# A hybrid decoder layer on one core: rows of the stationary operands at pitches over 1024 bytes

## The chip, the cores and the metric

The kernel runs on one core of a Trainium2 chip. The metric is the device time of one execution in microseconds. TensorE (PE) multiplies: for each matmul a weight load puts 128 columns of a stationary operand into the array, and then up to 512 columns of a moving operand stream through it; the result goes to a bank of PSUM. VectorE (DVE), ScalarE (ACT) and GpSimd (POOL) work elementwise, SyncE (SP) and POOL issue the loads. All operands of the engines lie in SBUF, 128 partitions of some 224 KiB; a place in it is given here as a byte within the partition.

## The reference

One layer on 256 tokens of width 1024, all in float32. Attention (8 heads of 64, causal within one block of 256 tokens) and a convolution module stand side by side, and a SwiGLU feed-forward of width 2816 follows:

```python
h = rms_norm(x, norm1_g[l])
proj = h @ w_in[l]                                  # 1024 x 2560
q, k, v, u = jnp.split(proj, [ATTN_WIDTH, 2 * ATTN_WIDTH, 3 * ATTN_WIDTH], axis=-1)
...
attn = moba_attention(...)                          # one block: causal softmax attention
conv = conformer_conv(u, ...)                       # GLU, 31-tap causal depthwise conv, layer norm, silu
x = x + jnp.concatenate([attn, conv], axis=-1) @ w_out[l]
h = rms_norm(x, norm2_g[l])
x = x + (jax.nn.silu(h @ w_gate[l]) * (h @ w_up[l])) @ w_down[l]
```

## The kernel before, in words

Every float32 product is made of three float32r products: each operand is split into a rounded high part and a rest (`xh`/`xl`, `mixh`/`mixl`, `wh`/`wl` and so on), and `high*high`, `high*low` and `low*high` are summed in PSUM (line 698 in the first projection, `product` with line 735 in all later ones). The activations are the stationary operands, in 128x128 blocks (one k-tile of 128 features by one of the two halves of the tokens), and the weights are the moving ones, 512 columns at a time. One matmul is therefore 128x512, and there are six for each k-tile and 512 columns of weights.

The stages in order, with the names of their results in PSUM and of their stationary operands:

- `p`: the first projection, 5 chunks of 512 columns, 8 k-tiles, 240 matmuls on `xh`, `xl` (line 698). The work of attention and convolution runs beside it in small tasks that a step counter starts: scores `S`, transposes `qT`, `kT`, `pT`, the convolution's spectrum `hf` on the constant `fwd` (lines 296 to 298).
- `O` (attention's output) and `cv` (the convolution's inverse transform, on the constant `inv`, lines 296 to 298, and one matmul on `tapr`, line 648).
- `po`: the output projection, 96 matmuls on `mixh`, `mixl`. These reuse the memory of `xh`, `xl` (tags `big_h`, `big_l`).
- `fg`, `U`, `V`, `W`: gate and up projections. The feed-forward's input is `g2` (high parts in `ffn["h"]`, rests in `ffn["l"]`, 8 rows each). Two of the six column blocks are done plainly (`fg`, 144 matmuls); the other four as seven products instead of eight of 2x2 blocks (`shared_unit`, `U`, `V`, `W`): three of the seven take blocks of `g2` (144 matmuls), the other four take sums and differences of blocks, `xs` (192 matmuls). In before, two of the four sums lie in the last four rows of `act`, which are filled only at the end, and two in a tile of their own, so half of these matmuls carry the name `act` in the profile.
- `pd`: the down projection, 264 matmuls on `act`, the split and transposed activations (22 rows of high parts, 22 of rests).

The order of the matmuls is written out (`TURNS`, `_order`), with the down projection's rows between the shared products. The weights come in 1 MB blocks (`raw`), from SP's queue; ACT makes `wh` (line 273) and DVE `wl` (line 278), some pieces ahead (`feed`). For the shared products POOL's queue adds one block of weights to another in memory (line 286). `SCRATCH` is the room, in bytes of each partition, that is set aside at the start of SBUF for the descriptors of POOL's queue.

The weight load of a matmul runs while the matmul ahead of it streams. In before all rows of the stationary operands have a pitch of 1024 bytes (256 float32), their two token halves lie 512 bytes apart, and every piece of weights starts 320 bytes over a multiple of 1024, in steps of 2048:

| tile | start, modulo 512 | pitch of its rows | place against the moving operand, modulo 512 |
|---|---|---|---|
| `wh`, `wl` (moving) | 320 | 2048 (halves) | - |
| `xh`, `xl`, `mixh`, `mixl`, `g2`, `act`, `xs` | 320 | 1024 (`xs`: 512) | 0 |
| `fwd`, against `hh`, `hl` | 416 | 1024 | 96 |
| `inv`, against `yh`, `yl` | 384 | 1024 | 64 (32 where `tapr` is next) |

Of the kernel before, what the change touches and what calls it, by code (L numbers as in the profile page):

```python
# [9 lines left out]
F32R = mybir.dt.float32r  # L10
# [6 lines left out]
P = 128  # L17
D = 1024
T = 256
NT = T // P  # L20
KT = D // P
# [4 lines left out]
NF = FF // P  # L26
# [25 lines left out]
LATE = (1, 5)  # L52
SECOND = 3
SCORES = 8
SCRATCH = 8192
GLU0_WAIT = 3
L1 = 8
L2 = 28
# [129 lines left out]
def build(nc, tc, t):  # L188
    with ExitStack() as ctx:
        _build(nc, tc, t, ctx)  # L190
    keep_order(nc, tc)


def _build(nc, tc, t, ctx):
    pool = lambda name, bufs=1, **kw: ctx.enter_context(tc.tile_pool(name=name, bufs=bufs, **kw))
    const = pool("const")
    keep = pool("keep")
# [6 lines left out]
    def mm_bank(name, two):  # L204
        return psum.tile([P, 512], F32, name=name, tag=f"mm{two}", bufs=2)
# [34 lines left out]
    def load(i):  # L240
        if i in homes:
            pl = late_pool[0] if homes[i] == "side" else keep
            r = pl.tile([P, BW], F32, name=f"raw{i}", tag=homes[i])
        else:
            r = raw.tile([P, BW], F32, name=f"raw{i}", tag="raw")
        nc.sync.dma_start(r, t["w"][i - 2])
        blocks[i] = r
# [94 lines left out]
        nc.tensor.matmul(warm[:, 0:T], zeros[:, 0:P], zeros, start=True, stop=True)  # L342


    xh = keep.tile([P, KT, T], F32R, name="xh", tag="big_h")
    xl = keep.tile([P, KT, T], F32R, name="xl", tag="big_l")
    def split_x(kt):
        nc.scalar.activation(xh[:, kt, :], xT[kt], AF.Copy, scale=g1[:, kt:kt + 1])
        yield
        nc.vector.scalar_tensor_tensor(xl[:, kt, :], xT[kt], g1[:, kt:kt + 1], xh[:, kt, :].bitcast(F32),  # L350
                                       op0=ALU.mult, op1=ALU.subtract)
        yield
# [40 lines left out]
    G = {}  # L393
# [311 lines left out]
    nc.scalar.activation(vs[:, 0, :], banks[0], AF.Copy, scale=rstd1[:, 0:1])  # L705
    nc.scalar.activation(vs[:, 1, :], banks[1], AF.Copy, scale=rstd1[:, 1:2])
    G["third"]()
    mix = G["mix"] = [keep.tile([P, KT, T], F32R, name="mix" + s, tag="big_" + s) for s in "hl"]
    O = [mm_bank(f"O{n}", 1).rearrange("p (a q) -> p a q", a=2) for n in range(2)]
    for second in range(2):  # L710
        step()
        for i in range(NT):
            for n in range(2):
                for odd in range(2):
                    h = 4 * n + 2 * second + odd
# [12 lines left out]
    ffn = {"r": None}  # L728
# [41 lines left out]
    at = 20  # L770
# [7 lines left out]
        at += 1  # L778
    early_ctx.close()
    late = ffn["late"] = late_pool[0] = pool("late")  # L780
    xg = late.tile([P, 2, KT, T], F32R, name="g2")
    ffn["h"], ffn["l"] = xg[:, 0], xg[:, 1]
    ffn["full"] = late.tile([P, KT, T], F32, name="full", tag="side")
    for n in range(2):
        for i in range(NT):
# [8 lines left out]
    spawn(turn_task(1), TURN_WAIT)  # L794


    acts = late.tile([P, 2, NF, T], F32R, name="act")
    load(first_shared[0])
    load(first_shared[2])

# [41 lines left out]
    def part(name):  # L842
        return late.tile([P, W], F32, name=name, tag="sum", bufs=4)

    more = late.tile([P, 2, 2, 4, P], F32R, name="xs")
    spare = [acts[:, z, NF - 4:, :].rearrange("p f (b q) -> p (f b) q", b=2).rearrange("p (s k) q -> p s k q", s=2)
             for z in range(2)]
    xs = [[(spare[z], more[:, z])[j // 2][:, j % 2] for j in range(4)] for z in range(2)]

    def xsums_task():  # L850
        a = ffn["full"]
# [178 lines left out]
```

## Time and profile before

| | |
|---|---|
| median of 2 runs | 283.17 us (282.84 and 283.5) |
| the profiled execution's own time | 282.85 us |
| its span, first to last instruction | 281.1 us |
| granted TensorE clock, mean | 1.000 |
| matmul records | 1302 |
| weight loads of pd from act (min/median/max) | 187/188/190 ns |
| ACT's wh, each 128x1024 | 1057 ns |
| DVE's wl, each 128x1024 | 1220 ns |
| packets of POOL's queue | 2848, 9.94 MB |

The span is what the trace covers; the execution's own time holds a little more around it. "Busy" of PE counts each matmul from its start to the modelled end of its drain, which overlaps the next one: a matmul of 389 ns does not hold the array for 389 ns. What counts is the distance from one start to the next, and that is read from the timeline's starts or from the chain of waits, whose rows give the time that a run of matmuls took and their number.

### The profile page before, as it was taken

The numbers are of one execution on the slowest core, as the hardware profiler recorded it, in microseconds if no ns is written. First come the engines' busy times: TensorE is split into PE (matmuls) and PEld (weight loads), VectorE is DVE, ScalarE is ACT, GpSimd is POOL, SyncE is SP. The second block draws the span as 40 slices with busy tenths as digits, with TensorE's granted clock in tenths as the row PEclk, the third lists the DMA queues.
The fourth block names the chain that finished last, engine by engine and source line by source line (L and its number), as shares of the span: only waits on it lengthen the run. The fifth ranks groups of instructions, "written<-read, shape, count | busy, mean of one in ns | idle before, by whom it ended". The sixth has DMA issues, their size and how long they took to land.

```text
span 281.1 us, 3712 instructions
## 1 busy us (share of the span) xinstructions
PE 276.5 (98%) x1302; PEld 225.8 (80%) x1302; DVE 238.5 (85%) x353; ACT 188.6 (67%) x280; POOL 30.5 (11%) x54
## 2 busy tenths in 40 slices
PE   8999999999999999999999999999999999999995
PEld 5878887888788888888888888888888888888883
DVE  3889998898994957999998999989998999978412
ACT  6768577998838778664887559765687568954300
POOL 0004555002000000011200012001110022000000
PEclk9999999999999999999999999999999999999999
DMA  7999967655543689349999689997699985910012
GB/s 240 412 415 325 411 217 266 239 215 161 223 150 149 234 295 368 133 169 212 264 243 361 266 209 193 349 426 215 108 177 423 373 189 96 328 58 2 0 53 97
DMA packets 13029, 65.12 MB, mean 232 GB/s; under 512 B 1841, under 2 KB 2705, under 8 KB 7250
## 3 DMA queue, kind: packets, MB, share of 16 engines
q1 hardware_dynamic: 9874, 54.80, 51.6%
q0 software_dynamic: 2848, 9.94, 19.0%
q8 instruction: 10, 0.16, 0.2%
q10 hardware_dynamic: 288, 0.14, 0.2%
q14 instruction: 9, 0.07, 0.1%
HBM read 63.63 MB, written 1.05 MB: 230 GB/s over the span
## 4 chain that ended last, share of the span: by engine, by line
PE 92%; DMA 4%; DVE 1%; issue 1%; SPq 0%; ACT 0%; DVEq 0%
PE pd L735 21%; PE U L735 16%; PE p L698 15%; PE fg L735 12%; PE po L735 8%; PE V L735 8%; PE W L735 4%; DMA c_gqk<-gqk 3%; PE aT L816 2%; DMA first<-first 1%; PE S L533 1%; PE O L717 1%; PE pT L567 1%; PE x2T L758 1%; PE cv L296 0%
## 5 line engine op out<-in xcount | busy, mean ns | idle before, releaser
L273 ACT ACTIVATE wh<-raw 128x1024 fp32r<-128x1024 f32 x114 | 117.8, 1057 | 35.8 <-DVE raw L272 19.9
L278 DVE TENSOR_TENSOR wl<-raw,wh 128x1024 fp32r<-128x1024 f32 x114 | 136.0, 1220 | 5.4 <-ACT wh L273 4.5
L735 PE MATMUL pd<-wh,act 128*128 128x512 f32 x176 | 58.0, 394 | 0.0
L735 PEld LDWEIGHTS pd<-wh,act 128*128 128x128 f32 x176 | 33.0, 188 | 6.8
L735 PE MATMUL pd<-wl,act 128*128 128x512 f32 x88 | 34.3, 389 | 0.0
L698 PE MATMUL p<-wh,xh 128*128 128x512 f32 x80 | 32.7, 408 | 0.0
L698 PE MATMUL p<-wh,xl 128*128 128x512 f32 x80 | 31.3, 391 | 0.0
L286 POOL DMA_DIRECT2D raw<-w x16 | 14.1, 880 | 157.7 <-PE fg L735 60.8
L735 PE MATMUL fg<-wh,g 128*128 128x512 f32 x96 | 30.4, 391 | 0.0
L698 PE MATMUL p<-wl,xh 128*128 128x512 f32 x80 | 26.6, 394 | 0.1
L735 PE MATMUL U<-wh,g 128*128 128x512 f32 x64 | 21.5, 393 | 0.0
L735 PEld LDWEIGHTS fg<-wh,g 128*128 128x128 f32 x96 | 18.0, 188 | 3.7
L272 DVE TENSOR_TENSOR raw<-raw,raw 128x1024 f32<-128x1024 f32 x16 | 19.5, 1219 | 0.1
L735 PEld LDWEIGHTS pd<-wl,act 128*128 128x128 f32 x88 | 16.6, 188 | 3.3
L735 PE MATMUL fg<-wl,g 128*128 128x512 f32 x48 | 18.7, 390 | 0.0
L698 PEld LDWEIGHTS p<-wh,xh 128*128 128x128 f32 x80 | 15.1, 189 | 3.8 <-issue 0.7
L698 PEld LDWEIGHTS p<-wl,xh 128*128 128x128 f32 x80 | 15.0, 189 | 3.7 <-DVE wl L278 0.7
L698 PEld LDWEIGHTS p<-wh,xl 128*128 128x128 f32 x80 | 15.0, 188 | 3.1
L819 ACT ACTIVATE act<-aT 128x512 fp32r<-128x512 f32 (+1 forms) x12 | 6.7, 560 | 12.9 <-PE aT L816 12.9
L735 PEld LDWEIGHTS U<-wh,g 128*128 128x128 f32 x64 | 12.0, 188 | 2.4
L735 PE MATMUL po<-wh,mixh 128*128 128x512 f32 x32 | 12.6, 395 | 0.0
L735 PE MATMUL po<-wh,mixl 128*128 128x512 f32 x32 | 12.5, 390 | 0.0
(184 smaller groups left out, 443.9 us busy)
## 6 DMA issues: line engine op xcount, KB each, us to landing
raw<-w SPq DMA_DIRECT2D x45, 1024.0 KB, 7.2
raw<-w POOLq DMA_DIRECT2D x16, 512.0 KB, 7.0
first<-first SPq DMA_DIRECT2D x8, 384.0 KB, 5.9
xtok<-xtok SPq DMA_DIRECT2D x2, 512.0 KB, 9.1
x<-xtok SPq DMA_DIRECT2D x2, 512.0 KB, 6.4
inv<-inv POOLq DMA_DIRECT2D x1, 768.0 KB, 5.3
out<-o SPq DMA_DIRECT2D x3, 256.0 KB, 2.0
c_glub<-glub SPq DMA_DIRECT2D x1, 512.0 KB, 10.4
```

Source lines behind the costliest of these rows:

```text
L272: nc.vector.tensor_tensor(src, src, blocks[add][:, cut(a)], op=ALU.add)
L273: nc.scalar.activation(dst[0], src, AF.Copy)
L278: nc.vector.tensor_tensor(dst[1], src, dst[0].bitcast(F32), op=ALU.subtract)
L286: nc.gpsimd.dma_start(blocks[to][:, cut(a)], t["w"][more - 2][:, cut(a)], accum_op=ALU.add)
L533: nc.tensor.matmul(banks[2 * j + a][:, out], G["qT"][rows, j, q], G["kT"][rows, j, k], start=True, stop=True)
L567: nc.tensor.transpose(b[:, a * P:(a + 1) * P], p[:, a * P:(a + 1) * P], ident)
L698: nc.tensor.matmul(banks[i], (xh, xh, xl)[a][:, kt, sls[i]], w[a % 2], start=kt == 0 and a == 0, stop=kt == KT - 1 and a == 2 - (order[-1] ...
L717: nc.tensor.matmul(o, vs[:, i, h * HD:(h + 1) * HD], G["pT"][h][:, i * T:i * T + T - i * P], start=i == 0, stop=i == 1)
L735: nc.tensor.matmul(bank, l, r, start=start and a == 0, stop=stop and a == 2, skip_group_check=on)
L758: nc.tensor.transpose(b[:, a, tok(i)], x2[:, i, k * P:(k + 1) * P], ident)
L816: nc.tensor.transpose(b[:, a, :], u[:, a * P:(a + 1) * P], ident)
L819: nc.scalar.activation(hi, b[:, 0:nf, :], AF.Copy)
```

## The change

Five rows of constants are new, and a helper `spaced` makes a tile whose rows of 256 elements have a number of unused elements behind each (and, for `mix`, 64 ahead of the first). `xh`, `xl` and `mix` get 8 (a pitch of 1056 bytes), `g2` gets 1 (1028 bytes), `act` gets 4 (1040 bytes). The four shared sums lie in a tile of their own, `more`, with rows of 512 bytes; the last rows of `act` are no longer lent to them. The room for POOL's descriptors is halved. Nothing is computed in another way, and the order of the instructions on all five engines is the same; only the names and places of operands differ.

```diff
-SCRATCH = 8192
+SCRATCH = 4096
+X_PAD = 8
+MIX_PAD = 8
+MIX_AT = 64
+G_PAD = 1
+ACT_PAD = 4
...
-    xh = keep.tile([P, KT, T], F32R, name="xh", tag="big_h")
-    xl = keep.tile([P, KT, T], F32R, name="xl", tag="big_l")
+    def spaced(pl, name, rows, pad, at=0, dt=F32R, **kw):
+        tl = pl.tile([P, at + rows * (T + pad)], dt, name=name, **kw)
+        return tl[:, at:].rearrange("p (k q) -> p k q", k=rows)[:, :, 0:T]
+
+    xh = spaced(keep, "xh", KT, X_PAD, tag="big_h")
+    xl = spaced(keep, "xl", KT, X_PAD, tag="big_l")
...
-    mix = G["mix"] = [keep.tile([P, KT, T], F32R, name="mix" + s, tag="big_" + s) for s in "hl"]
+    mix = G["mix"] = [spaced(keep, "mix" + s, KT, MIX_PAD, MIX_AT, tag="big_" + s) for s in "hl"]
...
-    xg = late.tile([P, 2, KT, T], F32R, name="g2")
-    ffn["h"], ffn["l"] = xg[:, 0], xg[:, 1]
+    xg = spaced(late, "g2", 2 * KT, G_PAD)
+    ffn["h"], ffn["l"] = xg[:, 0:KT], xg[:, KT:]
...
-    acts = late.tile([P, 2, NF, T], F32R, name="act")
+    acts = spaced(late, "act", 2 * NF, ACT_PAD).rearrange("p (z f) q -> p z f q", z=2)
...
-    more = late.tile([P, 2, 2, 4, P], F32R, name="xs")
-    spare = [acts[:, z, NF - 4:, :].rearrange("p f (b q) -> p (f b) q", b=2).rearrange("p (s k) q -> p s k q", s=2)
-             for z in range(2)]
-    xs = [[(spare[z], more[:, z])[j // 2][:, j % 2] for j in range(4)] for z in range(2)]
+    more = late.tile([P, 2, 4, 4, P], F32R, name="xs")
+    xs = [[more[:, z, j] for j in range(4)] for z in range(2)]
```

The places after the change, against the moving operand of the matmul during which the weight load runs, modulo 512 bytes:

| tile | place against the moving operand |
|---|---|
| `xh`, `xl` | 0 to 224 in steps of 32, by k-tile |
| `mixh`, `mixl` | 256 to 480 in steps of 32 |
| `g2` | 0 to 60 in steps of 4 (rests 32 above the high parts) |
| `act` | 0 to 496 in steps of 16 (rests 352 above the high parts) |
| `xs` | 256, all |

## The prediction

> **What bounds the kernel now.** I read the page's engine totals and clock first, then its chain of waits by line, then the same chain in order of time, and last single matmuls.
>
> ```profile
> PE 276.5 (98%) x1302; PEld 225.8 (80%) x1302; DVE 238.5 (85%) x353; ACT 188.6 (67%) x280; POOL 30.5 (11%) x54
> PEclk9999999999999999999999999999999999999999
> PE 92%; DMA 4%; DVE 1%; issue 1%; SPq 0%; ACT 0%; DVEq 0%
> PE pd L735 21%; PE U L735 16%; PE p L698 15%; PE fg L735 12%; PE po L735 8%; PE V L735 8%; PE W L735 4%; DMA c_gqk<-gqk 3%; PE aT L816 2%; DMA first<-first 1%; PE S L533 1%; PE O L717 1%; PE pT L567 1%; PE x2T L758 1%; PE cv L296 0%
> ```
>
> TensorE carries 92% of the chain at the full granted clock, and 84% lies on its 512-wide float32r matmuls (pd, U, p, fg, po, V, W). No engine feeds it late after the first 20 us. So the time is a number of matmuls times the spacing from one start to the next. The change alters nothing else on that chain, and the whole question is what the spacing does. The chain in order of time shows it (start, us, what, count):
>
> ```profile
> 20.23 12.99 PE p L698 x56
> ...
> 58.42 2.76 PE p L698 x12
> ...
> 69.08 1.39 PE p L698 x6
> ...
> 88.15 12.29 PE po L735 x54
> ...
> 107.65 20.42 PE fg L735 x90
> ...
> 136.70 0.44 PE aT L816 x4
> 137.13 5.49 PE fg L735 x24
> ...
> 154.00 2.72 PE V L735 x12
> ...
> 162.17 0.44 PE aT L816 x4
> 162.60 2.77 PE pd L735 x12
> ...
> 210.35 2.72 PE W L735 x12
> 213.07 2.72 PE pd L735 x12
> ...
> 265.29 12.30 PE pd L735 x54
> ```
>
> Long stretches keep one pace: 20.42/90 = 226.9 ns, 2.72/12 = 226.7 ns, the same for every tile. Behind an interruption (the transposes aT, 0.44 us) the matmuls are slower for a while: 2.77/12 = 230.8 ns, and where interruptions come every six matmuls, 1.39/6 = 231.7 ns. So there is a settled pace, 226.7, and an unsettled one near 231.7, and the same operands run at both.
>
> **What the places do, as far as this trace shows.** While a matmul streams 512 columns of its moving operand, the weight load of the next one runs beside it. In before, almost every such pair lies a multiple of 512 bytes apart. The exceptions are the convolution's matmuls: the rows of fwd lie 96 bytes further on (hf), those of inv 64 bytes (cv; 32 for the one that takes tapr). First one row for each form (durations min/median/max in ns), then starts from the timeline:
>
> ```profile
> L735 PE MATMUL pd<-wl,act x88: 387/389/397, 151.3 to 277.0; 128*128 128x512 f32 x88
> L698 PE MATMUL p<-wh,xl x80: 387/389/408, 5.7 to 71.8; 128*128 128x512 f32 x80
> L297 PE MATMUL cv<-yl,inv x5: 393/397/398, 75.4 to 78.5; 128*128 128x512 f32 x4, 121*128 121x512 f32 x1
> L297 PE MATMUL hf<-hl,fwd x4: 391/396/400, 64.7 to 68.5; 128*128 128x512 f32 x4
> ```
>
> ```profile
> 64.67 0.39 PE L297 MATMUL hf<-hl,fwd 128*128 128x512 f32 x1
> ...
> 65.83 0.39 PE L698 MATMUL p<-wh,xh 128*128 128x512 f32 x1
> ...
> 66.97 0.39 PE L698 MATMUL p<-wh,xl 128*128 128x512 f32 x1
> ...
> 67.75 0.40 PE L297 MATMUL hf<-hl,fwd 128*128 128x512 f32 x1
> ...
> 68.92 0.39 PE L698 MATMUL p<-wh,xh 128*128 128x512 f32 x1
> ```
>
> ```profile
> 75.44 0.40 PE L297 MATMUL cv<-yl,inv 128*128 128x512 f32 x1
> ...
> 78.95 0.39 PE L735 MATMUL po<-wh,mixh 128*128 128x512 f32 x1
> ```
>
> hf: five spacings take 65.83 - 64.67 = 1.16 us (232 ns), and 68.92 - 67.75 = 1.17 us (234 ns). The p matmuls between them, back at multiples of 512, take 66.97 - 65.83 = 1.14 us for five, 228 ns, at once. cv: fifteen spacings, uninterrupted, take 78.95 - 75.44 = 3.51 us, 234.0 ns. Fifteen are enough to settle elsewhere; the fg row behind the transposes at 136.70 has 5.49 - 24 x 0.2267 = 0.05 us left over in all, which ten unsettled ones use up. So cv never settles. Over these 25 spacings the mean is (1.16 + 1.17 + 3.51)/25 = 233.6 ns. Could busy neighbours be the cause? No:
>
> ```profile
> 76.00:78.90 2.90, 2.90 (x14) 2.36 (x13) 2.90 (x4) 2.90 (x5) 0.00 (x0) 1.00 0.01 3
> 110.00:131.00 21.00, 21.00 (x94) 17.41 (x93) 20.05 (x35) 14.31 (x20) 1.83 (x2) 1.00 0.54 178
> ```
>
> Columns: window and length; busy time of PE, PEld, DVE, ACT, POOL; clock; DMA share; GB/s. DVE is as good as full in both stretches, and DMA nearly idle in the slow one.
>
> **The change part by part.**
>
> Rows of xh/xl (pitch 1056 bytes), mix (1056, and 256 bytes on), g2 (1028) and act (1040): the weight load's place now differs from the moving operand's by another amount at almost every row. Nothing that settles is left, except where a row happens to lie right. I take 233.6 ns, from the rows that it is nearest to, for all of them; the unsettled pace at equal places, 231.7, is the lower end. Counts are from the page's groups.
> - p, 240 matmuls: already 230.0 (2.76/12) to 232.0 (12.99/56), about 231. +2.6 x 240 = 0.6 us.
> - po, 96: 12.29/54 = 227.6 now. +6.0 x 96 = 0.6 us.
> - on g2, 288 (fg 144, W 48, and the 96 of U that read g): 226.7 to 228.8, about 227.1. +6.5 x 288 = 1.9 us.
> - pd, 264: 12.30/54 = 227.8 now. +5.8 x 264 = 1.5 us.
>
> All of this is on the chain, undiluted: PE has no idle time there that could take it up. DVE, ACT and the loads get a little more room.
>
> Shared sums in their own tile xs, 192 matmuls: all of them now lie 256 bytes (or 768) from the moving operand. The trace has 0 and 512, not 256. Ends: 0, and 192 x 6.9 = 1.3 us. I take 0.4 us: they settle as at 0, but some twelve groups of them, of 12 or 24 matmuls, follow others that are unsettled, and each walks in anew at (231.7 - 226.7) x 7, or 0.035 us. The last four rows of act are no longer read by them; the waits at these instructions are on the same engines as before, so nothing starts earlier.
>
> Writers of these rows: mix is now written as two rows of 256 where it was 512 in one run. act was always written as four separate rows, and costs the same, so this is zero:
>
> ```profile
> L255 DVE TENSOR_TENSOR mixl<-O,mixh x2: 681/686/692, 75.6 to 76.2; 128x512 fp32r<-128x512 f32 x2
> L821 DVE TENSOR_TENSOR act<-aT,act x12: 418/684/692, 137.9 to 266.0; 128x512 fp32r<-128x512 f32 x10, 128x256 fp32r<-128x256 f32 x2
> ```
>
> Half the room for descriptors of POOL's queue (8192 to 4096 bytes): its 16 added loads issue in 0.88 us each, and it idles long between them. Zero; if POOL did wait for room, the additions to raw would come late, and ACT's wh behind them.
>
> ```profile
> L286 POOL DMA_DIRECT2D raw<-w x16 | 14.1, 880 | 157.7 <-PE fg L735 60.8 <-DMA raw<-w 42.3 <-DVE wl L278 28.8
> ```
>
> Sum: 0.6 + 0.6 + 1.9 + 1.5 + 0.4 = 5.0 us. The profiled execution took 282.85 us (0.32 under the median of the two shown, 283.17), so 287.8 us. With 231.7 ns it is 0.2 + 0.4 + 1.3 + 1.0 + 0.4 = 3.3 us, 286.2; with 235.3, and the sums unsettled too (1.3), 5.0 + 888 x 0.0017 + 0.9 = 7.4 us, 290.3.
>
> **The rivals.**
>
> 1. Places have no effect. Then cv's slow run is a walk that took unusually long, and the time stays at 283.2. For it: equal places show both paces, so something else sets them at least in part. Against it: p settles at once between two hf groups that do not. The Trainium skill says so outright: "SBUF — State Buffer", section "Who interferes with whom", gives TensorE two read ports, one for the moving operand and one for weight loads, calls them independent, and states that PE waits on nobody. By that rule the sum would be 0 and the time 283; the cv rows (234.0 against 226.7 ns) speak against it here, though only with 25 spacings.
>
> 2. Faster: the settled pace is itself held up, as both reads meet at the same place in every pair, and variety frees it. For it: 226.7 is not a floor, since single matmuls have 387 ns where the settled ones have 389. The 888 average 228.4 ns now (the four terms' paces by their counts); at 2 ns less than 226.7 they save 888 x 3.7 = 3.3 us: 279.6. Against it: the hf and cv rows above have no duration under 391. How far it could go no row shows. The Trainium skill, "TensorE: Matmul & The Clock Gate", section "Back-to-back issue gap", has N/2.4 + 2.5, or 215.7 ns, for 512 columns; with it the estimate would be 283 - 888 x 0.0127 = 272.
>
> 3. Slower still: no stationary row of the trace starts off a multiple of 32 bytes; those of g2 now lie 4 apart and those of act 16. If such a load costs what the longest uninterrupted matmul shows (408 ns against 389, or 19 more, 12 above my 6.9), g2 adds 288 x 12 = 3.5 us, act 264 x 12 = 3.2: 291.3 to 294.5.
>
> **How the numbers follow.** Forecast 0.50, no effect 0.20, faster 0.20, slower still 0.10. The time of the likeliest is 287.8, its own range 286 to 290.5. About 2% (277.5 to 288.8) is what a measurement of this kernel can tell from no change. Of the forecast's chance some 0.32 lies under 288.8 and 0.18 above; of the faster case 0.06 lies above 277.5. Faster 0.14; within 0.20 + 0.06 + 0.32 = 0.58; slower 0.18 + 0.10 = 0.28. The range runs from 279.5 (most of the faster case lies below, 0.15) to 292.5 (0.05 above).
>
> **What would show it.** In the chain in order of time, rows of 12 uninterrupted matmuls on g2, act and mix at 2.78 to 2.82 us, where 2.72 stands now; rows of U and V on xs at 2.72 to 2.75; six p matmuls at 1.40. Median durations of pd, fg and po near 396, of xs at 389. Rival 1 keeps 389 everywhere; rival 2 has medians under 387; rival 3 has g2's rows apart from act's and p's, over 400. The forecast is wrong if the groups on g2, act and mix settle at one pace although their places vary, or if another engine's row enters the chain after 20 us.

## The result, and the profile after

The changed kernel takes 286.13 us (median of 2 runs, 286.07 and 286.19) where the one before takes 283.17: 1.0111 times as long, 95% interval 1.0092 to 1.0131. That is slower, by less than the 2% that were set as the bound. 287.8 was forecast, with 286.2 as the sum at the lower end of the unsettled pace. The profiled execution's span grew from 281.1 to 284.4 us.

Engine totals and chain by line of the changed kernel, from the page:

```profile
PE 279.9 (98%) x1302; PEld 226.0 (79%) x1302; DVE 238.7 (84%) x353; ACT 189.0 (66%) x280; POOL 30.5 (11%) x54
...
PE 98%; DVE 0%; DVEq 0%; issue 0%
PE pd L744 22%; PE p L707 20%; PE U L744 16%; PE fg L744 12%; PE po L744 8%; PE V L744 8%; PE W L744 4%; PE aT L825 2%; PE warm L347 1%; PE S L542 1%; PE O L726 1%; PE pT L576 1%; PE x2T L767 1%; PE cv L301 0%; PE cv L302 0%; PE cv L303 0%
```

The other engines' busy time is what it was (DVE 238.5 before, ACT 188.6, POOL 30.5), and PE's is 3.4 us more. That p has 20% of the chain where it had 15% is no cost: in before the chain goes back through the first loads until 20.23 us, here through TensorE, and the 64 matmuls of p that start before then lose nothing. The chain in order of time (start, us, what, count) says where:

```profile
67.76 0.33 PE pT L576 x3
...
69.48 1.39 PE p L707 x6
...
88.70 12.59 PE po L744 x54
...
108.61 20.79 PE fg L744 x90
...
138.62 5.53 PE fg L744 x24
...
173.19 2.72 PE V L744 x12
175.91 2.72 PE U L744 x12
178.63 2.78 PE W L744 x12
181.41 2.80 PE pd L744 x12
184.21 2.72 PE U L744 x12
186.93 2.72 PE V L744 x12
189.65 2.79 PE pd L744 x12
192.44 2.79 PE U L744 x12
...
268.39 12.57 PE pd L744 x54
```

Read the rows of 12. W, pd and the U at 192.44 work on g2 and act: 2.78 to 2.80 us where 2.72 stood. V and U between them work on the shared sums xs: 2.72 us, the settled pace, as before. The single runs of po, fg and pd went from 12.29, 20.42 and 12.30 us to 12.59, 20.79 and 12.57. The loss is found in every stage whose rows moved, and is next to nothing (0.2 us over 192 matmuls) where the place is the same in every row and a multiple of 256 bytes. The sharpest view of it is one tile's matmuls (durations min/median/max in ns), first U on g2 in before, then U and pd in the changed kernel:

```profile
L735 PE MATMUL U<-wh,g x64: 389/389/476, 127.9 to 257.2; 128*128 128x512 f32 x64
```

```profile
L744 PE MATMUL U<-wh,g x64: 387/393/481, 129.2 to 260.2; 128*128 128x512 f32 x64
L744 PE MATMUL U<-wh,xs x64: 387/389/482, 144.0 to 251.9; 128*128 128x512 f32 x64
```

```profile
L744 PE MATMUL pd<-wh,act x176: 387/394/483, 152.6 to 280.5; 128*128 128x512 f32 x176
L744 PE MATMUL pd<-wl,act x88: 388/394/400, 153.0 to 280.3; 128*128 128x512 f32 x88
```

The same result tile U now has a median of 393 ns with stationary blocks from g2, where it had 389, and 389 with blocks from xs. A duration here is the spacing to the next start plus about 162 ns (389 against 227, 393 against 231).

### The profile page after: what moved, and what is told of

It is laid out like the page before. It is cut to its first block, busy times and chain, and to the rows that moved or that the text cites. A ratio compares the mean times of both kernels' runs of the same rounds, so it can differ in the third digit from the quotient of the medians.

```text
span 284.4 us, 3712 instructions
## 1 busy us (share of the span) xinstructions
PE 279.9 (98%) x1302; PEld 226.0 (79%) x1302; DVE 238.7 (84%) x353; ACT 189.0 (66%) x280; POOL 30.5 (11%) x54
## 4 chain that ended last, share of the span: by engine, by line
PE 98%; DVE 0%; DVEq 0%; issue 0%
PE pd L744 22%; PE p L707 20%; PE U L744 16%; PE fg L744 12%; PE po L744 8%; PE V L744 8%; PE W L744 4%; PE aT L825 2%; PE warm L347 1%; PE S L542 1%; PE O L726 1%; PE pT L576 1%; PE x2T L767 1%; PE cv L301 0%; PE cv L302 0%; PE cv L303 0%
## 5 line engine op out<-in xcount | busy, mean ns | idle before, releaser
L744 PE MATMUL pd<-wh,act 128*128 128x512 f32 x176 | 58.6, 398 | 0.0
L744 PE MATMUL V<-wh,xs 128*128 128x512 f32 x64 | 21.4, 392 | 0.0
L744 PE MATMUL U<-wh,xs 128*128 128x512 f32 x64 | 21.3, 391 | 0.0
```

The lines of the kernel that those rows point to most:

```text
L744: nc.tensor.matmul(bank, l, r, start=start and a == 0, stop=stop and a == 2, skip_group_check=on)
```

## The experiments

Three theories were left by the trace. A: a stationary row whose place changes from one to the next keeps the matmuls from settling, and any constant place would settle at 226.7 ns. B: each place has a pace of its own, and 0 is a good one. C: the halved room for descriptors or the own tile of the sums carries part. In all the kernels below but the last (n3) the tiles keep sizes of a multiple of 512 bytes, so that only the stated places differ.

**The first four: taking the pads away, and constant places.**

```diff
 e1_no_pads
-X_PAD = 8; MIX_PAD = 8; MIX_AT = 64; G_PAD = 1; ACT_PAD = 4
+all pads 0, all rows start where the tile starts
 e2_pitch_1280, against e1_no_pads
+X_PAD = 64; MIX_PAD = 64
 e3_ffn_64, against e1_no_pads (elements of 4 bytes ahead of the first row)
+X_AT = 32; MIX_AT = 8; G_AT = 16; ACT_AT = 16; XS_AT = 16
 e4_ffn_128, against e1_no_pads
+X_AT = 8; MIX_AT = 4; G_AT = 32; ACT_AT = 32; XS_AT = 32
```

> All pads taken away, the halved room for POOL's descriptors and the own tile of the shared sums kept; every stationary row lies at 0 modulo 512 against the moving operand again. Theory A (only a place that changes from row to row unsettles the matmuls) and theory B (each place has a pace of its own, and 0 has 226.7 ns): 283.2 us, within 0.6, and rows of 12 matmuls at 2.72 us on xs, g2 and act alike. Theory C (the other two parts carry some of the 3 us): 284 to 286 us.

> As the run without pads, but xh, xl and mix have rows at a pitch of 1280 bytes, so that their places alternate between 0 and 256. A pitch over 1024 bytes by itself, or theory A with any change of place at all: p and po stay unsettled at about 232 ns, 284.4 us, and the 54 matmuls of po in one run take 12.5 us. Theory B with 256 as good as 0: 283.2 us, and these 54 take 12.27 us.

> Rows at a pitch of 1024 bytes again, so that the places stay the same from row to row, but not at 0: xh and xl at 128, mix at 32, g2, act and xs at 64. Theory A: all settle at 226.7 ns, 283.2 us. Theory B, with the convolution's 234 ns for 64: 744 matmuls of the feed-forward part cost 6 to 7 ns more each, 288 us, and 12 of them take 2.80 us.

> Places constant again: xh and xl at 32, mix at 16, g2, act and xs at 128. Theory A: 283.2 us. Theory B has a pace for each: if 128 is as good as 0 and 256, 283 to 284.5 us with 12 matmuls of the feed-forward part at 2.72 us; if it is as 64, 287 to 288 us at 2.79 us.

| kernel | median, us | ratio to before, 95% interval |
|---|---|---|
| before, in the same runs | 282.85 | |
| e1_no_pads | 282.89 | 1.0 (0.9991 to 1.001) |
| e2_pitch_1280 | 282.83 | 1.0001 (0.999 to 1.0011) |
| e3_ffn_64 | 288.5 | 1.0201 (1.0184 to 1.0218) |
| e4_ffn_128 | 287.89 | 1.0185 (1.0169 to 1.02) |

C falls: without the pads nothing of the 3 us is left. A falls too: rows that keep one constant place, 64 or 128, do not settle at 226.7 ns, and cost more than the changing rows of the change. In e2 rows whose places alternate between 0 and 256 cost nothing, so a pitch over 1024 bytes is no cost in itself. As 256 is as good as 0, e2 does not show what an alternation between a good place and a bad one would cost. The chain of e2_pitch_1280, whose po alternates:

```profile
88.14 12.29 PE po L745 x54
...
107.64 20.41 PE fg L745 x90
```

The chain of e3_ffn_64 (mix at 32; g2 and act at 64):

```profile
89.80 12.59 PE po L745 x54
...
109.75 21.00 PE fg L745 x90
...
271.37 12.61 PE pd L745 x54
```

21.00/90 = 233.3 ns, against 20.41/90 = 226.8. Those ninety matmuls have no interruption, and in the trace's starts they alternate 236 and 231 ns from the third on: a mean pace that does hold, only a slower one. What counts is the place against the moving operand. It is given modulo 256 bytes from here on, because 0 and 256 are alike; that other places repeat after 256 bytes was not tried.

**A map of the places.** Twelve more places in three kernels, each constant, and one kernel that moves everything; all edits are against e1_no_pads.

```diff
 m1_48_80_96_112
+X_AT = 12; MIX_AT = 20; G_AT = 24; ACT_AT = 28; XS_AT = 28
 m2_144_160_176_192
+X_AT = 36; MIX_AT = 40; G_AT = 44; ACT_AT = 48; XS_AT = 48
 m3_208_224_240_4
+X_AT = 52; MIX_AT = 56; G_AT = 60; ACT_AT = 1; XS_AT = 1
 m4_all_moved
+    shift = const.tile([P, 16], F32, name="shift")
+    nc.vector.memset(shift, 0.0)
```

> Constant places, pitch 1024: xh and xl at 48, mix at 80, g2 at 96, act and xs at 112. Theory B1 (0 and 256 alone keep 34 steps of 6.67 ns; every other place ends at 35 steps or wanders about it): each of the four at 232 to 234 ns, 288 us. Theory B2 (the pace depends on the place with a wider good region, or better places): one or more of the four at or under 227, and the time 1 to 5 us less than 288.

> The same with xh and xl at 144, mix at 160, g2 at 176, act and xs at 192. B1: 232 to 234 ns in all four, 288 us. B2: one or more at or under 227 ns.

> The same with xh and xl at 208, mix at 224, g2 at 240 (16 under 256), act and xs at 4, which is no multiple of 16. B1: 232 to 234 ns in all four, 288 us; rival 3 of the prediction: act and xs at 4 near 246 ns, 294 us. B2: one or more at or under 227 ns.

> No pads, and one more small constant of 64 bytes ahead of everything, so that moving and stationary operands all lie 64 bytes further on and keep their place against each other. If the place against the moving operand is what counts: 283 us, 226.7 ns. If it is where the stationary rows lie in the partition: 288 us and 233.3 ns, as with 64 in the run before.

One run each: 288.39, 286.75, 286.75 and 283.57 us, with before at 282.43 beside them. m4 is 1.1 us over that one run of before; its matmuls are not the reason, as its chain shows:

```profile
88.89 12.29 PE po L747 x54
...
108.39 20.42 PE fg L747 x90
...
266.03 12.30 PE pd L747 x54
```

These are the settled rows of before to 0.01 us; its chain only reaches them 0.74 us later, before any matmul of po. In m4 the stationary rows start 128 bytes over a multiple of 256, and so do the moving ones; in e3_ffn_64 the rows of g2 and act start at the same 128, with the moving ones at 64, and fg has 233.3 ns. So it is the place against the moving operand that counts, not where the rows lie. This is shown for a step of 64 bytes; for the other places of the map it is assumed.

**Just beside 0.**

```diff
 n1_252_248_8_12, against e1_no_pads
+X_AT = 63; MIX_AT = 62; G_AT = 2; ACT_AT = 3; XS_AT = 3
```

> Constant places just beside 0, pitch 1024: xh and xl at 252 (4 under 256), mix at 248, g2 at 8, act and xs at 12. If 0 is a single good place: 230 to 234 ns in all four, 286 to 288 us. If the pace falls off gradually from 0, as 240 with 228.3 suggests: under 229 ns at 252, 248 and 8, near 284 us. A place better than 0: under 226 ns in one of them.

287.5 us in one run, with before at 283.02 beside it. There is no gradual slope down to 0: 252 and 248 stand at 233.4 ns, 8 at 230.6. All places together, as mean spacing of the matmuls that come 12 or more behind an interruption, worked out from the starts in the traces:

| place modulo 256 | mean spacing, ns | tile and kernel |
|---|---|---|
| 0 (also 256) | 226.7 | all, in before, e1, e2, m4 |
| 4 | 232.5 | act, m3 |
| 8 | 230.6 | g2, n1 |
| 12 | 231.6 and 231.2, of 230.0 and 233.3 | act and xs, n1 |
| 16, 32, 48, 64 | 233.2 to 233.4 | mix e4; mix e3, xh e4; xh m1; g2 e3 |
| 80 | 232.0 | mix, m1 |
| 96 | 234.3 | g2, m1 |
| 112 | 233.3 | act, m1 |
| 128 | 232.4 | g2, e4 |
| 144, 160 | 233.4 | xh, mix, m2 |
| 176 | 230.3 | g2, m2 |
| 192 | 231.3 and 232.0, of 228.9 and 233.3 | act and xs, m2 |
| 208 | 231.9 | xh, m3 |
| 224 | 233.3 | mix, m3 |
| 240 | 228.2 | g2, m3 |
| 248, 252 | 233.4 | mix, xh, n1 |

B1 holds to a part. No place is better than 0, so B2's hope of a faster one falls for these places, and 0 stands alone. But the others do not all lie at 232 to 234: 8, 176 and 240 are between. Nor has each place one pace of its own, as B says. At 12 and at 192 the means are mixtures of two paces, each kept for a dozen matmuls and more, on the same operands in the same run. In n1:

```profile
216.60 2.76 PE pd L745 x12
...
247.90 2.80 PE pd L745 x12
```

In the first row the spacings alternate 224 and 236 ns, in the second they are 233 and 234. So a place alone does not fix the pace there; what decides between the two, perhaps how the matmuls come in from the row ahead, no run here isolates.

The map also gives the size of the change. Averaged over the places that each tile's rows now have, with 233.3 ns for those of g2 that were not measured, it says 232.4 ns for xh and xl, 232.3 for mix, 232.2 for act and 232.5 for g2. The changed kernel's trace has 232.4, 232.3, 231.9 and 231.4. This is an estimate, and for g2, most of whose places were not measured, it is 1.1 ns too high.

**What the weight load does to the stream.** If it is the load's walk through memory that meets the stream's, a load that stands still should behave otherwise. This edit makes every load from po to pd read its first column 128 times. What it computes there is the first token's result for all tokens of a half.

```diff
 n2_one_column, against e1_no_pads; n3_one_column_pads, against the changed kernel
-            nc.tensor.matmul(bank, l, r, ...)
+            nc.tensor.matmul(bank, l[:, 0:1].to_broadcast([P, P]), r, ...)
```

> No pads, and the weight loads from po to pd read one column 128 times instead of 128 columns, so that a load stays at one place of 4 bytes while the stream passes (all tokens of a half get the first one's result). Theory M1 (a load and the stream hold each other up where they are in the same part of a 256-byte round at the same time): the pace of po, fg, U, V, W and pd changes, most likely to 32 or 33 steps of 6.67 ns (213 to 220), 277 us or less. Theory M2 (128 reads beside the stream cost what they cost, wherever they lie, and the place only shifts the rounding): 226.7 ns and 283 us.

> The changed kernel with its pads, and weight loads that read one column 128 times as in the run before. M1: the rows' places no longer matter as they did; the time is within 1 us of the run before. M2: 3 us over the run before, with 231 to 232 ns on g2, act and mix.

285.37 us (1.0082 of before, 1.0051 to 1.0112) and 286.57 us (1.0124, 1.0091 to 1.0157). The chain of n2_one_column:

```profile
88.66 12.51 PE po L745 x54
...
108.49 20.60 PE fg L745 x90
...
267.79 12.39 PE pd L745 x54
```

and of n3_one_column_pads:

```profile
89.06 12.51 PE po L744 x54
...
108.89 20.63 PE fg L744 x90
...
268.65 12.54 PE pd L744 x54
```

Neither theory got its pace. With M1 it should have become faster, with M2 it should have stayed; it became slower, 228.9 ns in fg where 226.8 stood, and no longer settles. M1 also foresaw the two runs within 1 us of each other; they are 1.2 us apart. po and fg are alike with and without the pads (12.51 and 12.51; 20.60 and 20.63), where walking loads had 12.29 against 12.59 and 20.41 against 20.79. pd keeps 0.15 us of its 0.27. From start to start, 1.0 us lies between the two traces. Of it 0.4 us is p's, whose loads still walk and which has its pads in the second: its spacings, those with a wait left out, average 229.0 and 232.4 ns. Another 0.4 lies on act, and 0.2 on xs, whose place is 0 in the first and 256 in the second. So on mix and g2 the places act through the walk of the load along its row; for act that is shown in part only, and what xs loses is not explained. A walk at place 0 is better than no walk at all. Why, these runs don't settle.

## Why the prediction was right, and where its sizes were off

- **The bound and the term that matters.** As predicted: nothing but the spacing of the 512-wide matmuls changed, and after 20 us no other engine's row came into the chain.
- **The pace of moved rows, 233.6 ns.** This is the term that was mis-sized. It was taken from hf and cv, whose places are constant (96, 64, 32), and for constant places it is right: e3_ffn_64 holds 233.3. But the rows of the change differ among themselves, and such a mixture averages less, as a part of the rows lies at 0 or another of the better places: 231.4 ns on g2, 231.9 on act, 232.3 on mix, 232.4 on xh, from the trace's starts. Medians of pd, fg and po are 392 to 396 ns where 396 was foreseen, rows of 12 take 2.75 to 2.82 us where 2.78 to 2.82 was. The lower end of the range, 231.7 ns and 286.2 us, meets the measured time to 0.1 us, and that is luck. It is the pace of matmuls at place 0 behind interruptions, which no run ties to the pace of mixed places, and its terms for p (0.2) and xs (0.4) miss the measured 0.4 and 0.2 in opposite directions. For the upper end's 235.3 ns no row is shown; the slowest place tried has 234.3. The nearest row was nearest in the kind of place and not in the kind of sequence.
- **"p settles at once between two hf groups."** This reading, the argument against rival 1, took the better of two cases. Behind the first hf group five spacings of p take 1.14 us; behind the second, the six at 69.08, at the same place 0, take 1.39 us, or 231.7 ns. So it says little about places, and the choice between the forecast and rival 1 rested on hf and cv alone. Of the 25 spacings behind 233.6 ns, three end at a row at place 0 (the last of each stretch); without them it is 233.5.
- **By stage.** po 0.5 us against 0.6 forecast (8.17, 12.29 and 1.38 became 8.32, 12.59 and 1.40). On g2 288 x (231.4 - 227.0) = 1.3 against 1.9. pd 264 x (231.9 - 227.8) = 1.1 against 1.5. xs 192 x (228.0 - 226.9) = 0.2 against 0.4. p 0.4 against 0.6: the p row behind the second hf group begins 0.4 us later than before (69.48 against 69.08). Here two errors work against each other. p's pace was not about 231 but 229 ns, since 12.99 us for 56 holds a wait (the first spacing is 338 ns), and it became 232.3, so that each matmul lost 3 ns and not 2.6; but 64 of the 240 start before 20.23 us, where they wait for loads, and lost nothing. Together 3.5, of the span's 3.3.
- **The sums at 256 settle.** Right, and it was a guess between two ends: the trace had only 0 and 512. e2_pitch_1280 shows why, as 256 is as good as 0.
- **"Nothing that settles is left" because places vary from row to row.** The outcome was right and the reason was not. A varying place is harmless if it is always 0 or 256 (e2), and constant places away from 0 are worse than the varying ones of the change (288.5 and 287.9 against 286.1 us).
- **Rival 1, no effect.** Refuted, by 5.6 us in e3_ffn_64, whose instructions are those of e1_no_pads. The Trainium skill's "SBUF — State Buffer", section "Who interferes with whom", calls the two read ports of TensorE independent and says that PE waits on nobody; here the place of one read against the other moves the pace by 3%, and the measurement decides.
- **Rival 2, variety frees the pace.** Refuted for the twenty places tried: none holds a pace under 226.7 ns, though single spacings of 224 occur.
- **Rival 3, rows off a multiple of 32 bytes.** Refuted: 4, 8 and 12 have 232.5, 230.6 and 231.2 to 231.6, no more than 16 to 64.
- **Zero-priced parts.** The halved room for descriptors and the own tile of the sums together: 282.89 against 282.85 us. Writing mix in two rows of 256: within that of e2, where it is written so too.

## What to carry to other kernels

Where matmuls stream 512 float32r columns back to back, each with a weight load beside it, lay the stationary rows and the moving rows at the same place modulo 256 bytes: here that is worth 1.1% against the mixed places of the change and 2% against a constant 64, and it is free. A tuned kernel may have it by accident, through tiles whose sizes are all multiples of 512 bytes; a pad that has another purpose should then be a multiple of 256. When a price is taken from rows that resemble the new case, ask in which respect they do: in this case constant and mixed places differ by as much as a third of the whole effect.

## What the runs showed of the hardware that was not expected

Two paces are held with spacings that differ by no more than 1 ns: 226.67 (226 and 227 in turn, at place 0) and 233.33 (233 and 234, at 112, 248 and 252, and in a part of the rows at 12 and 192). They are 34 and 35 times their own difference of 6.67 ns; whether that is a step of the hardware no run shows. The other means belong to short cycles of spacings between 224 and 241 ns that repeat to 1 ns, such as 229, 226, 229, 236 at 176, and 236, 231 at 64, whose mean is 233.3 as well. At 12 and 192 both a lower cycle (230.0 and 228.9 ns) and 233.3 are kept. Behind an interruption the spacings at place 0 mostly walk through one and the same sequence (... 233, 236, 224, 231, 236, 228, 233, 231, then 226.7), give or take 1 ns, but enter it at different points. In before fg settles after two such spacings at 107.7 us and after eight at 137.2. And a weight load that reads one column over and over is no relief to the stream: 228.9 ns in fg, against 226.8 with loads that walk in step with it.
